# The value projection of a gated linear attention layer by seven products: where its steps stand between the q and k items, and when the sums of x are made

## The chip, the cores and the metric

The kernel runs on one core of one Trainium2 chip. The metric is the device time of one execution in microseconds. The kernel before took 1250.46 us (median of 3 runs, 1249.15 to 1251.29). A difference of 0.2%, 2.5 us, is about what a measurement of it can tell from no change.

The core's engines have names in the profile: PE multiplies matrices (PEld is its weight load), DVE works on vectors, ACT evaluates functions and copies, POOL works on vectors too and issues DMAs that can add to what is in memory, SP only issues DMAs. Each engine takes its instructions in the order that the build leaves: that of the program, in which a scheduler moves what is not held in place.

## The reference

Two layers, each a token mixer and a channel mixer (a gated feed-forward block with a short convolution). The change lies in the first mixer, gated linear attention, and in the reading of x ahead of it.

```python
def gla_mixer(x, w_in, w_gk2, b_gk, norm_w, w_out):
    proj = x @ w_in                                  # x: 512 x 1024
    q, k, v, gate, gk_lr = jnp.split(proj, [hk, 2 * hk, 2 * hk + hv, 2 * hk + 2 * hv], axis=-1)
    gk = jax.nn.log_sigmoid((gk_lr @ w_gk2 + b_gk).astype(jnp.float32)) / GLA_NORMALIZER
    ...
    o = rms_norm(gla_chunked(qc, kc, vc, gc), norm_w)
    o = from_head_chunks(o).astype(x.dtype)
    return (o * jax.nn.silu(gate)) @ w_out
```

All of it is float32. q and k have 4 heads of 128 columns each, v and gate 1024 columns, gk_lr 16.

## The kernel before, in words

**Two parts for each number.** A float32 matrix is kept as a high part in a rounded format that PE takes fast and a low part, the rest: xh and xl for x, wh and wl for a weight. A product is three matmuls: wh xh, wh xl and wl xh. To make a weight ready, a DMA brings the raw tile, ACT casts it to wh (L343, L285) and DVE subtracts to get wl (L346, L286). For some items the low part is made another way (L336 to L338): ACT casts wh, ACT writes minus the raw tile, rounded, into wl (L337), and POOL issues a DMA that adds the raw tile to it (L338); the plan says which items, by its argument `bydma`.

**Start.** x comes in four blocks of 128 tokens (tb 0 to 3). PE transposes a block (`tr4`, tile xT), ACT and DVE make xh and xl from it (`x_parts`). Blocks 0 and 1 come first; `second()` is a task that does blocks 2 and 3 while PE is already at work on the first weights. The first four q and k items (i0 to i3) run on the first half of the tokens, then on the second half. The build keeps its own clock, `self.clk`, an estimate; a task says with `yield` how long it sleeps on that clock, so such numbers and the order of the statements fix where a task's instructions come among the others.

**The order of the GLA projection.** After i0 to i3, the string `GLA_ORDER` fixes the order of PE's work: an `i` is an item, an `s` a step of the value projection. The first `i` is the narrow gk_lr item ("lr" below), the others are i4 to i7, each 24 matmuls of 512 columns (tile fm). In the middle of an item or a step the task `prepare(hd)` puts one matmul for the decay of a head (tile z) and after it a chain on ACT and DVE: z, na (exp and ln on ACT), a scan on DVE (bc), differences and exponentials e1, e2, e4, e5 and bc on ACT, and products with q and k on DVE.

**v by seven products.** x and the columns of w_in for v are cut in 2 by 2 blocks. Instead of 8 block products there are 7, with sums of x's blocks on one side and of the weight's blocks on the other. The weight's sums are made by DMAs on POOL that add to a tile in place (L243, tile wq); x's sums are tiles sf and x1. Its 14 steps s0 to s13 are `sums_proj`: s0 to s3 are the first phase, s4 to s7 the second, s8 to s11 the third, the last two the fourth. A step is 12 matmuls of 512 columns. A phase adds into two pairs of PSUM banks, A and B (tile tm). When its last step is done, `onto_v` reads the banks: for v's first parts by ACT (L1170, tile v), for the others by DVE (L1172). The next phase goes on adding in bank A and B, without clearing, so its first matmul in a bank may only come after that read.

**x's sums.** `x_whole` makes xh + xl of blocks 0 and 1 by four additions on POOL (tiles x1), ahead of the transposes of blocks 2 and 3. `x_sums`, called from `x_parts` right after each transpose, forms x1 minus the even chunks of the transpose (sf "3") and minus that minus the odd ones (sf "2") on DVE. `x_split` adds them to the x1 tiles and makes the high and low parts (tiles sh and sl) that the steps read.

**How far ahead weights are made ready** is `self.look`: 3 at the start, set to `LOOKAHEAD` = 2 by `second()` once blocks 2 and 3 are done, and by `gla` after the items. High and low parts have 4 buffers each, raw tiles 3.

The lines that the prediction names: L180 is every matmul, L191 every transpose, L598 a split in high and low part, L650 the additions on POOL, L660 and L661 the sums on DVE, L678 and L683 the additions of `x_split`, L285, L286, L336 to L338, L343 and L346 the weights' parts, L243 the adding DMAs, L313 a load of a raw tile for the products behind v, L1131 the exponential e1, L1170 ACT's reads of the banks. The change shifts line numbers behind x_sums by 4 at most.

Of the kernel before, what the change touches and what calls it, by code (L numbers as in the profile page):

```python
# [13 lines left out]
ALU = mybir.AluOpType  # L14
# [15 lines left out]
GDN_SCALE = 128.0 ** -0.5  # L30
CHUNKS = ((0, 3), (3, 6), (6, 9))
PLAIN = (9, 11)
GLA_ORDER = "iississsisssissssss"
HALF = 2 * P
AHEAD = 3
BYDMA = 1
# [3 lines left out]
LOOKAHEAD = 2  # L40
TAIL = 4
HEADSTART = 4
# [9 lines left out]
def c4(t):  # L52
    return t.rearrange("p (c i) -> p c i", c=4)


def pairs(t):
    return t.rearrange("p (c i) -> p c i", c=2)


def blk(i, n=P):  # L60
    return slice(i * n, i * n + n)


class Trunk:
# [565 lines left out]
    def x_parts(self, tb):  # L630
        for hf in range(2):
            ps = self.psum("xT")
            self.tr4(ps, self.h[tb][hf])
            xs = (slice(None), slice(4 * hf, 4 * hf + 4), blk(tb))
            self.split_out(self.xh[xs], self.xl[xs], c4(ps))
            if tb > 1:
                self.x_sums(ps, tb - 2, hf)
        self.set(("x", tb))

    def x_whole(self):  # L640

        nc = self.nc
        self.x1 = []
        self.sf = [{k: self.slot("sf") for k in "23"} for _ in range(2)]
        for hf in range(2):
            row = []
            for odd in range(2):
                t = self.slot("x1")
                at = slice(None), slice(4 * hf + odd, 4 * hf + 4, 2), slice(0, HALF)
                nc.gpsimd.tensor_add(pairs(t), self.xh[at], self.xl[at])  # L650
                row.append(t)
            self.x1.append(row)

    def x_sums(self, ps, j, hf):

        nc = self.nc
        p3 = c4(ps)
        even, odd = p3[:, 0::2, :], p3[:, 1::2, :]
        at = slice(None), slice(None), blk(j)
        nc.vector.tensor_sub(pairs(self.sf[hf]["3"])[at], pairs(self.x1[hf][0])[at], even)  # L660
        nc.vector.scalar_tensor_tensor(pairs(self.sf[hf]["2"])[at], pairs(self.sf[hf]["3"])[at], -1.0, odd,  # L661
                                       ALU.mult, ALU.subtract)

    def x_split(self):

# [28 lines left out]
    def load_x(self, x):  # L694

        nc = self.nc
        self.h = [[self.slot("h") for _ in range(2)] for _ in range(NTB)]

        def load(eng, tb):
            for hf in range(2):  # L700
                self.tc.keep_in_program_order(eng.dma_start(self.h[tb][hf], x[blk(tb), blk(hf, S)]))

        def constant(n):
            for _ in range(n):
                self.tc.keep_in_program_order(nc.tensor.matmul(ps, self.ident, self.reset, start=True, stop=True))

        load(nc.sync, 0)
        load(nc.scalar, 1)

        _, w, col, _ = self.plan[0]  # L710
        self.raw = self.rp.tile([P, 1024], F32, name=self.uid("raw"), tag="raw")
        for i, eng in enumerate((nc.sync, nc.scalar)):
            self.tc.keep_in_program_order(eng.dma_start(
                self.raw[:, blk(i, S)].rearrange("p (c f) -> p c f", c=NC // 2),
                w[blk(i, S), col:col + P].rearrange("(c p) f -> p c f", p=P)))

        self.tc.keep_in_program_order(nc.scalar.copy(self.warm, self.one))
        ps = self.psum("warm")
        constant(2)
        self.hold = True  # L720
        for tb in range(2):
            self.x_parts(tb)
        constant(2)
        self.tc.keep_in_program_order(nc.sync.dma_start(self.mark[:, 0:1], self.h[0][1][:, 0:1]))
        self.look = 3
        self.prefetch()
        for tb in range(2, NTB):
            load(nc.sync, tb)
        self.hold = False

        def second():
            self.x_whole()
            yield 5.5
            for tb in range(2, NTB):
                self.x_parts(tb)
                yield 1.2
            self.look = LOOKAHEAD
            yield 4.0
            self.h = [[None] * 2 for _ in range(NTB)]
            yield from self.x_split()  # L740

        self.spawn(second(), 0.5)

    def reload(self, x):

# [296 lines left out]
    def gla_plan(self, w_in, w_out):  # L1042
        items = iter([base + hd * P for hd in range(GH) for base in (0, 512)])
        sums = self.sums_plan(w_in, range(0, NC, 2), 1024)
        for k, kind in enumerate("i" * HEADSTART + GLA_ORDER):
            if k == HEADSTART:
                self.plan_rep(w_in, 3072)
            elif kind == "i":
                self.plan_fm(w_in, next(items), k > HEADSTART + 2)
            else:  # L1050
                self.plan.append(next(sums))
        for hf in range(2):
            for cp in range(NC // 2):
                self.plan_tm(w_in, 2 * cp * P, 2, 2048 + hf * S)
        self.plan_out(w_out, 0, NC, TAIL)
# [29 lines left out]
    def gla(self, x, li, g, b):  # L1085
# [92 lines left out]
        def steps():  # L1178
            self.wait("combined")
            yield from self.sums_proj(self.xs, onto_v)  # L1180
            self.xs = None

        self.look = 3
        self.fm_items(items, steps(), GLA_ORDER)
        self.look = LOOKAHEAD
# [565 lines left out]
```

## Time and profile before

| | us |
|---|---|
| median of 3 runs | 1250.46 |
| the profiled execution | 1254.08 |
| its span, first to last instruction | 1252.4 |
| PE busy in the span | 1233.4 |
| DVE busy | 878.3 |
| ACT busy | 641.9 |
| POOL busy | 188.6 |

How to read it: the profile is one execution, 3.6 us longer than the median of the runs, and 1.7 us of it lie outside the span. PE is busy nearly all the time, so what counts are the few places where PE waits, and those where its clock is halved. The view of the waits names, for each engine and line, whom it waited for, the sum in us, how often, and the longest. The windows give the busy time of each engine in a stretch and the granted clock of PE (PEclk, 1.00 is full). The timeline lists instructions in order of time as start, duration, engine, line, operation, tiles, with the idle time before and what ended it in brackets; x2 means that two such instructions follow each other. A duration in the timeline overlaps the next by about 0.1 us on ACT and DVE and 0.16 us on PE, so start to start is what one costs in a row.

### The profile page before, as it was taken

The page shows a single profiled execution, that of the slowest core. Times are in us where ns is not written, and L with a number is a line of the kernel's source. Part 1 is how long each engine was busy: PE and PEld are TensorE (multiplying, and loading weights), DVE is VectorE, ACT ScalarE, POOL GpSimd, SP SyncE. Part 2 cuts the span into 40 slices and gives each one's busy share as a digit, 9 for nine tenths or more (in the row PEclk, how much of TensorE's full clock was granted, in tenths as well). Part 3 has the DMA queues.
Part 4 walks back from the last instruction along what each step waited for, and adds up shares of the span by engine and source line. Part 5 has one row for each costly group of instructions (what it writes and reads, how often), then busy time and mean ns, then how long its engine had stood idle before and what let it go on. Part 6 is the DMA issues. An engine that isn't in the chain of part 4 may idle for free.

```text
span 1252.4 us, 17852 instructions
## 1 busy us (share of the span) xinstructions
PE 1233.4 (98%) x6512; PEld 1041.5 (83%) x6512; DVE 878.3 (70%) x1717; ACT 641.9 (51%) x1205; POOL 188.6 (15%) x264
## 2 busy tenths in 40 slices
PE   8989999999999999999999999999999999999997
PEld 7868888988888888888888889988888888888885
DVE  6667466588667666687698946669588766766677
ACT  3765443654454454555558745543554454453441
POOL 6230000012101101201013330200012201201201
PEclk9989999999999999999999999999999999999999
DMA  8882324069757756742345950333159666766923
GB/s 221 200 171 79 110 71 148 2 156 222 176 136 167 168 137 168 169 125 96 86 141 134 213 124 27 115 105 114 39 129 229 141 158 169 154 148 152 216 85 101
DMA packets 188679, 172.19 MB, mean 137 GB/s; under 512 B 19240, under 2 KB 142954, under 8 KB 188592
## 3 DMA queue, kind: packets, MB, share of 16 engines
q1 hardware_dynamic: 163728, 117.07, 31.2%
q0 software_dynamic: 23904, 53.07, 23.4%
q8 instruction: 51, 0.84, 0.3%
q10 hardware_dynamic: 960, 0.92, 0.2%
q14 instruction: 36, 0.29, 0.1%
HBM read 148.99 MB, written 5.78 MB: 124 GB/s over the span
## 4 chain that ended last, share of the span: by engine, by line
PE 94%; DVE 3%; DMA 1%; ACT 1%; issue 0%; SPq 0%; DVEq 0%; ACTq 0%
PE fm L180 53%; PE tm L180 31%; PE o L180 2%; PE xT L191 1%; PE R L180 1%; PE V L180 1%; PE yT L191 1%; PE pq L180 1%; PE pg L180 1%; PE vn L180 1%; DVE wl L346 1%; DMA raw<-in_ffn_w_in_dram 1%; PE qs L180 0%; PE s L180 0%; PE ks L180 0%
## 5 line engine op out<-in xcount | busy, mean ns | idle before, releaser
L180 PE MATMUL fm<-xh,wh 128*128 128x512 f32 (+1 forms) x1104 | 407.3, 369 | 0.1
L180 PE MATMUL fm<-xl,wh 128*128 128x512 f32 (+1 forms) x1104 | 402.9, 365 | 0.0
L180 PE MATMUL fm<-xh,wl 128*128 128x512 f32 (+1 forms) x1096 | 399.2, 365 | 1.8 <-DVE wl L346 1.8
L180 PEld LDWEIGHTS fm<-xh,wh 128*128 128x128 f32 x1104 | 208.9, 189 | 33.5 <-ACT wh L343 0.3
L180 PEld LDWEIGHTS fm<-xl,wh 128*128 128x128 f32 x1104 | 209.0, 189 | 32.9 <-issue 0.2
L180 PEld LDWEIGHTS fm<-xh,wl 128*128 128x128 f32 x1096 | 207.0, 189 | 34.9 <-DVE wl L346 2.0
L346 DVE TENSOR_TENSOR wl<-raw,wh 128x1024 fp32r<-128x1024 f32 (+1 forms) x115 | 141.8, 1236 | 113.6 <-ACT wh L343 112.6
L343 ACT CAST wh<-raw 128x1024 fp32r<-128x1024 f32 x113 | 118.7, 1051 | 184.6 <-PE fm L180 103.5
L285 ACT CAST wh<-wq 128x512 fp32r<-128x512 f32 x154 | 91.1, 619 | 106.2 <-PE fm L180 38.3
L928 DVE SCALAR_TENSOR_TENSOR conv<-fm,ffn_cw,conv 128x511 f32<-128x511 f32 (+1 forms) x176 | 131.1, 746 | 19.8 <-ACT conv L926 17.8
L286 DVE TENSOR_TENSOR wl<-wq,wh 128x512 fp32r<-128x512 f32 x154 | 103.2, 686 | 53.9 <-ACT wh L285 52.9
L243 POOL DMA_DIRECT2D wq<-in_ffn_w_out_dram x72 | 63.1, 907 | 264.8 <-DVE wl L286 151.9
L338 POOL DMA_DIRECT2D wl<-raw x31 | 27.4, 884 | 400.3 <-ACT wl L337 384.0
L180 PE MATMUL tm<-wh,gh 128*128 128x512 f32 x216 | 84.0, 389 | 0.0
L180 PE MATMUL tm<-wh,gl 128*128 128x512 f32 x216 | 84.0, 389 | 0.0
L180 PE MATMUL tm<-wl,gh 128*128 128x512 f32 x216 | 84.0, 389 | 0.0
L526 DVE TENSOR_TENSOR h<-h,tm 128x512 f32<-128x512 f32 x68 | 44.9, 681 | 35.4 <-PE tm L180 35.4
L180 PE MATMUL tm<-wh,xh 128*128 128x512 f32 x152 | 63.4, 418 | 0.0
L926 ACT ACTIVATE conv<-fm,ffn_cw 128x512 f32<-128x512 f32 x88 | 59.9, 683 | 1.3 <-PE fm L180 1.3
L180 PE MATMUL tm<-wh,xl 128*128 128x512 f32 x152 | 59.8, 394 | 0.0
L180 PE MATMUL tm<-wl,xh 128*128 128x512 f32 x152 | 59.7, 393 | 0.0
L1312 DVE SCALAR_TENSOR_TENSOR conv<-fm,gdn_cw,conv 128x511 f32<-128x511 f32 (+2 forms) x72 | 53.4, 745 | 7.3 <-ACT conv L1310 6.5
(325 smaller groups left out, 1964.8 us busy)
## 6 DMA issues: line engine op xcount, KB each, us to landing
raw<-in_ffn_w_in_dram SPq DMA_DIRECT2D x88, 512.0 KB, 4.9
wq<-in_ffn_w_out_dram SPq DMA_DIRECT2D x72, 256.0 KB, 5.6
wq<-in_ffn_w_out_dram POOLq DMA_DIRECT2D x72, 256.0 KB, 5.1
raw<-in_gdn_w_in_dram SPq DMA_DIRECT2D x32, 512.0 KB, 4.2
wl<-raw POOLq DMA_DIRECT2D x31, 512.0 KB, 4.8
raw<-in_gla_w_in_dram SPq DMA_DIRECT2D x15, 512.0 KB, 4.5
h<-in_ln_b_dram POOLq DMA_DIRECT2D x20, 256.0 KB, 6.8
wq<-in_gla_w_in_dram SPq DMA_DIRECT2D x16, 256.0 KB, 4.8
```

The lines of the kernel that those rows point to most:

```text
L180: t = self.nc.tensor.matmul(out, a, b, start=start, stop=stop, skip_group_check=open_group)
L191: t = self.nc.tensor.transpose(out, a, self.ident[:n, :n])
L243: nc.gpsimd.dma_start(t[i], quad(i, r, col), accum_op=ALU.add)
L285: nc.scalar.copy(wh, t)
L286: nc.vector.tensor_sub(wl, t, wh)
L338: nc.gpsimd.dma_start(wl.bitcast(F32), raw, accum_op=ALU.add)
L343: cast = nc.scalar.copy(wh[:, cols], raw[:, cols])
L346: low = nc.vector.tensor_sub(wl[:, cols], raw[:, cols], wh[:, cols])
L526: nc.vector.tensor_tensor(h, h, ps, op)
L926: nc.scalar.activation(a, ps, AF.Identity, scale=tap(2))
L928: nc.vector.scalar_tensor_tensor(a[:, d:], ps[:, :S - d], tap(2 - d), a[:, d:], ALU.mult, ALU.add)
L1312: self.conv = nc.vector.scalar_tensor_tensor(a[:, d:], ps[:, :S - d], tap(3 - d), a[:, d:], ALU.mult, ALU.add)
```

## The change

It moves four things.

- `GLA_ORDER`: item i6 goes from behind s4 to ahead of it, so that an item stands between the first and the second phase, as i7 stands between the second and the third in both.
- `x_sums` no longer needs x1: it takes xh minus the transpose, plus xl (three instructions in place of two), and runs after both transposes; `x_whole` comes after it. So the four additions on POOL go behind the transposes of blocks 2 and 3.
- `second()` no longer sets the look-ahead to 2, so it stays 3 until the items are done. The task starts at 6.0 in place of 0.5 on the build's clock.
- No item of the GLA layer has its low part made by DMA any more: i5, i6 and i7 get theirs by DVE, as i0 to i4.

```diff
-GLA_ORDER = "iississsisssissssss"
+GLA_ORDER = "iissississssissssss"
...
             if tb > 1:
-                self.x_sums(ps, tb - 2, hf)
+                self.xt.append((ps, tb - 2, hf))
...
     def x_whole(self):
...
         self.x1 = []
-        self.sf = [{k: self.slot("sf") for k in "23"} for _ in range(2)]
...
-    def x_sums(self, ps, j, hf):
+    def x_sums(self):
...
-        nc.vector.tensor_sub(pairs(self.sf[hf]["3"])[at], pairs(self.x1[hf][0])[at], even)
-        nc.vector.scalar_tensor_tensor(pairs(self.sf[hf]["2"])[at], pairs(self.sf[hf]["3"])[at], -1.0, odd,
-                                       ALU.mult, ALU.subtract)
+        self.sf = [{k: self.slot("sf") for k in "23"} for _ in range(2)]
+        for ps, j, hf in self.xt:
+            p3 = c4(ps)
+            at = slice(None), slice(None), blk(j)
+            s2, s3 = (pairs(self.sf[hf][k])[at] for k in "23")
+            xh, xl = (x[:, 4 * hf:4 * hf + 4:2, blk(j)] for x in (self.xh, self.xl))
+            nc.vector.tensor_sub(s3, xh, p3[:, 0::2, :])
+            nc.vector.tensor_add(s3, s3, xl)
+            nc.vector.scalar_tensor_tensor(s2, s3, -1.0, p3[:, 1::2, :], ALU.mult, ALU.subtract)
...
         def second():
-            self.x_whole()
-            yield 5.5
+            self.xt = []
             for tb in range(2, NTB):
                 self.x_parts(tb)
                 yield 1.2
-            self.look = LOOKAHEAD
-            yield 4.0
+            self.x_sums()
+            self.xt = None
+            yield 1.5
+            self.x_whole()
+            yield 5.0
             self.h = [[None] * 2 for _ in range(NTB)]
             yield from self.x_split()
 
-        self.spawn(second(), 0.5)
+        self.spawn(second(), 6.0)
...
             elif kind == "i":
-                self.plan_fm(w_in, next(items), k > HEADSTART + 2)
+                self.plan_fm(w_in, next(items))
```

The order in which the instructions stand moves on every engine, from the first transposes to the end of the GLA layer; from the first feed-forward block on it is the same as before.

On PE, at the end of s3 (tiles tm_110 and tm_111 are bank A, tm_115 and tm_116 bank B, fm_152 is item i6), before:

```order
L180 MATMUL tm_116_622<-wl_124_663,sh_83_485 128x512
L180 MATMUL tm_116_622<-wh_123_662,sl_84_486 128x512
L180 MATMUL tm_110_605<-wh_128_703,sh_71_404 128x512
L180 MATMUL tm_110_605<-wl_129_704,sh_71_404 128x512
L180 MATMUL tm_110_605<-wh_128_703,sl_72_405 128x512
L180 MATMUL tm_111_606<-wh_128_703,sh_71_404 128x512
```

And now (tm_118 and tm_119 are bank A, tm_121 is of bank B, z_153 is the decay of head 2):

```order
L180 MATMUL tm_121_643<-wl_124_657,sh_93_536 128x512
L180 MATMUL tm_121_643<-wh_123_656,sl_94_537 128x512
L180 MATMUL fm_152_796<-xh_58,wh_127_680 128x512
L180 MATMUL fm_152_796<-xl_59,wh_127_680 128x512
L180 MATMUL fm_152_796<-xh_58,wl_128_681 128x512
...
L180 MATMUL z_153_825<-lr_39_185,gk2_27_169 128x512
L180 MATMUL tm_118_634<-wh_135_723,sh_77_445 128x512
```

Before, the first matmul of s4 follows at once on the last of s3 and writes the bank that `onto_v` has to read; now the 24 matmuls of i6 and the one of z stand between them.

On ACT, around its reads of the banks after the first phase (v_140 to v_143; wh_144 is s5's weight, wh_150 s6's; e1_139 to bc_137 belong to the decay of head 1), before:

```order
L285 CAST wh_144_767<-wq_122_659 128x512
L1118 ACTIVATE na_132_718<-na_132_718 128x512
L1119 ACTIVATE na_132_718<-na_132_718,one_2_85 128x512
L285 CAST wh_150_800<-wq_87_507 128x512
L285 CAST wh_150_800<-wq_127_700 128x512
L1131 ACTIVATE e1_139_750<-e2_138_748 128x512
L1170 ACTIVATE v_140_753<-tm_110_605 128x512
L1132 ACTIVATE e2_138_748<-e2_138_748 128x512
L1170 ACTIVATE v_141_755<-tm_111_606 128x512
```

And now (wh_140 is s5's weight, wh_150 s6's):

```order
L285 CAST wh_140_749<-wq_122_653 128x512
L285 CAST wh_150_790<-wq_62_335 128x512
L1135 ACTIVATE e1_139_740<-e2_138_738 128x512
L285 CAST wh_150_790<-wq_125_675 128x512
L1136 ACTIVATE e2_138_738<-e2_138_738 128x512
L1140 ACTIVATE e4_142_761<-e4_142_761 128x512
L1146 ACTIVATE e5_143_764<-e5_143_764 128x512
L1147 ACTIVATE bc_137_736<-bc_137_736 128x512
L1174 ACTIVATE v_145_773<-tm_118_634 128x512
L1174 ACTIVATE v_146_775<-tm_119_635 128x512
```

The reads stand behind the exponentials of head 1 in both, in the new order behind all five.

On POOL, from the mask on (x1 tiles are the additions of `x_whole`, gk the weight of the decay, rows its bias, wq the weights of v), before:

```order
L1083 CAST gla_mask_31_176<-maskf_30_172 128x512
L650 TENSOR_TENSOR x1_49_207<-xh_58,xl_59 128x512
L650 TENSOR_TENSOR x1_50_209<-xh_58,xl_59 128x512
L650 TENSOR_TENSOR x1_51_211<-xh_58,xl_59 128x512
L650 TENSOR_TENSOR x1_52_213<-xh_58,xl_59 128x512
L1065 COPY mark_3_86<-h_12_104 128x1
L1067 DMA gk_59_311<-in_gla_w_gk2_dram 16x512 x6
L620 DMA rows_60_319<-in_gla_b_gk_dram 4x128
L243 DMA wq_62_329<-in_gla_w_in_dram 128x512
```

And now:

```order
L1087 CAST gla_mask_31_176<-maskf_30_172 128x512
L1069 COPY mark_3_86<-h_12_104 128x1
L1071 DMA gk_51_285<-in_gla_w_gk2_dram 16x512 x6
L620 DMA rows_52_293<-in_gla_b_gk_dram 4x128
L243 DMA wq_58_325<-in_gla_w_in_dram 128x512
L649 TENSOR_TENSOR x1_64_351<-xh_58,xl_59 128x512
L649 TENSOR_TENSOR x1_65_353<-xh_58,xl_59 128x512
L243 DMA wq_60_330<-in_gla_w_in_dram 128x512
L649 TENSOR_TENSOR x1_66_355<-xh_58,xl_59 128x512
L649 TENSOR_TENSOR x1_67_357<-xh_58,xl_59 128x512
```

The four additions have gone behind the first adding DMA of v's weights, and a second such DMA stands between them.

More of the change, by code (lines that the diff above doesn't have):

```diff
@@ L652, in x_whole @@
             self.x1.append(row)
-    def x_sums(self, ps, j, hf):
+    def x_sums(self):
         nc = self.nc
[L657 to L660, printed above, removed]
-        nc.vector.scalar_tensor_tensor(pairs(self.sf[hf]["2"])[at], pairs(self.sf[hf]["3"])[at], -1.0, odd,
-                                       ALU.mult, ALU.subtract)
+        self.sf = [{k: self.slot("sf") for k in "23"} for _ in range(2)]
[7 more added lines that the diff above has]
+            nc.vector.scalar_tensor_tensor(s2, s3, -1.0, p3[:, 1::2, :], ALU.mult, ALU.subtract)
     def x_split(self):
```

## Prediction

> **What bounds the kernel now.** First the page: the span and the busy times.
>
> ```profile
> span 1252.4 us, 17852 instructions
> PE 1233.4 (98%) x6512; PEld 1041.5 (83%) x6512; DVE 878.3 (70%) x1717; ACT 641.9 (51%) x1205; POOL 188.6 (15%) x264
> ```
>
> PE is busy for all but 19 us. The change neither adds nor takes a matmul, so it can gain only where PE waits or its clock is halved, and lose only by new waits. So I read next the waits of PE, all that there are.
>
> ```profile
> PE tm L180 <- ACT v L1170: 4.2, 1, 4.2
> PE warm L705 <- POOL reset L93: 2.0, 1, 2.0
> PE fm L180 <- DVE wl L346: 1.8, 1, 1.8
> PE xT L191 <- DVE ln_mv L779: 1.3, 1, 1.3
> PE tm L180 <- DVE gl L598: 0.4, 1, 0.4
> ```
>
> The first and third lie in the part that the change reorders. The windows, cut where the granted clock changes, show what follows each (start:end, length, then busy us of PE, PEld, DVE, ACT, POOL, then PEclk, DMA share, GB/s).
>
> ```profile
> 12.47:15.88 3.41, 1.62 (x14) 1.43 (x13) 3.41 (x2) 1.04 (x1) 3.41 (x3) 1.00 1.09 348
> 15.88:19.30 3.42, 3.42 (x19) 3.42 (x18) 1.63 (x2) 1.05 (x1) 3.42 (x3) 0.50 0.70 144
> 63.67:67.08 3.41, 0.50 (x3) 0.08 (x1) 3.02 (x4) 1.39 (x3) 1.41 (x3) 1.00 1.08 198
> 67.08:70.49 3.41, 2.12 (x5) 1.74 (x6) 3.00 (x7) 3.29 (x7) 1.49 (x2) 0.50 1.08 195
> 70.49:73.91 3.42, 3.42 (x9) 2.65 (x9) 2.54 (x7) 1.50 (x4) 0.00 (x0) 0.50 1.04 214
> 882.80:886.20 3.40, 2.08 (x12) 1.59 (x12) 2.82 (x12) 1.56 (x3) 0.00 (x0) 1.00 0.34 103
> 886.20:889.60 3.40, 3.40 (x23) 2.97 (x22) 2.40 (x5) 3.40 (x11) 0.00 (x0) 1.00 0.00 0
> ```
>
> After the stretch with 1.62 us of PE work comes half clock for 3.42 us; after that with 0.50 us two such stretches. The 1.3 us wait at 883 left 2.08 us of work in its stretch, and the clock stayed. So each of the two waits costs itself and a slow stretch.
>
> **The change part by part: i6 between s3 and s4.** The timeline of PE at the long wait, and one row of the chain of waits with s0 and s1 for the price of a matmul:
>
> ```profile
> 47.59 5.44 PE tm L180 x24
> 63.78 0.39 PE L180 MATMUL tm<-wh,sl 128*128 128x512 f32 x1
> 68.37 0.80 PE L180 MATMUL tm<-wh,sh 128*128 128x512 f32 x1 [4.20 <-ACT v L1170]
> 73.66 0.52 PE L180 MATMUL fm<-xh,wh 128*128 128x512 f32 x1
> ```
>
> A matmul costs 5.44/24 = 0.227 us from start to start. The next one was due at 64.01 and came at 68.37: 4.36 us. The 12 from there to 73.66 took 5.29 us where 12 x 0.227 = 2.72 are due: 2.6 us more by the half clock. What held it is on ACT:
>
> ```profile
> 64.21 1.14 ACT L285 CAST wh<-wq 128x512 fp32r<-128x512 f32 x2 [0.28 <-PE tm L180]
> 67.20 0.63 ACT L1131 ACTIVATE e<-e 128x512 f32<-128x512 f32 x1 [1.85 <-DVE e L1128]
> 67.73 0.58 ACT L1170 ACTIVATE v<-tm 128x512 f32<-128x512 f32 x1
> 68.21 0.62 ACT L1132 ACTIVATE e<-e 128x512 f32<-128x512 f32 x1
> 68.73 1.56 ACT L1170 ACTIVATE v<-tm 128x512 f32<-128x512 f32 x3
> ```
>
> The reads of the banks stand behind an exponential of head 1, which waits for its chain on DVE. In the new order PE has 24 matmuls of i6 and one z to do meanwhile, 25 x 0.227 = 5.7 us. Let T be the end of s3. ACT then has, one behind the other, a cast that waits for T, e1, a cast, e2, e4, e5 and bc, and then the reads. They follow each other at 68.73 - 68.21 = 0.52 us, so the first read ends at T + 8 x 0.52 = T + 4.2, needed at T + 5.7: 1.5 us to spare. It is less if e1 again waits for DVE. There e1 needs the low part of i6 (now on DVE), na, z, a scan, four low parts of 512 columns and a difference. By these rows,
>
> ```profile
> 33.13 1.23 DVE L346 TENSOR_TENSOR wl<-raw,wh 128x1024 fp32r<-128x1024 f32 x1 [1.16 <-ACT wh L343]
> 51.41 1.22 DVE L1123 TENSOR_TENSOR_SCAN bc<-reset,z 128x512 f32<-128x512 f32 x1
> 55.61 0.69 DVE L1147 TENSOR_TENSOR e<-e,qk 128x512 f32<-128x512 f32 x1
> 56.21 0.68 DVE L1148 TENSOR_TENSOR e<-e,qk 128x512 f32<-128x512 f32 x1
> ```
>
> that is 1.15 + 1.14 + 7 x 0.60 = 6.5 us (0.60 from 55.61 to 56.21, the long ones less 0.08 of overlap). Head 1's z now comes at the end of i5, some 7 us ahead of T, not within s2; following the rows from there, e1 begins about T + 1.2 in place of T + 0.5, and 0.8 us are left. So the wait goes, 4.36 + 2.6 = 7.0 us, with 0 to 0.8 us of a new one at that place. What is next late there would be the second read, 0.5 us behind the first and wanted 0.7 us after it, so none.
>
> **The additions leave DVE alone at the start.** The other wait is for DVE's low part of i1. The chain, DVE's and POOL's timelines, and the durations of the additions (min, median, max in ns):
>
> ```profile
> 12.15 2.27 DVE wl L346
> 12.15 4.48 DVE L346 TENSOR_TENSOR wl<-raw,wh 128x1024 fp32r<-128x1024 f32 x2 [1.59 <-ACT wh L343]
> 12.05 6.95 POOL L650 TENSOR_TENSOR x<-xh,xl 128x512 f32<-128x512 f32 x4
> L650 POOL TENSOR_TENSOR x<-xh,xl x4: 1266/1767/2260, 12.1 to 17.7; 128x512 f32<-128x512 f32 x4
> ```
>
> The low part that took 1.23 us at 33.13 with POOL idle takes 2.27 beside the additions, and it is on the path. Now POOL waits there for x's last block, so the low part takes 1.23: the wait shrinks by 1.04 us to 0.8. The stretch 12.47 to 15.88 then holds 1.62 + 1.04 = 2.66 us of PE work, more than the 2.08 that kept its clock at 883, so the half clock of 15.88 to 19.30 goes as well: 3.42/2 = 1.7 us. Together 2.7 us, after which PE is earlier by that much.
>
> The Trainium skill, "TensorE: Matmul & The Clock Gate", section "What's actually happening", says that the clock drops after at least one idle window of about 3.4 us. The row of 12.47 has 1.62 us of work and was still followed by half clock, so the measurement decides here; the rule is a rival below.
>
> **x's sums and the tight place behind them.** The additions now follow POOL's first adding DMA. One row of the chain of waits, and rows of the timelines and groups:
>
> ```profile
> 45.97 0.23 PE z L180
> 26.57 0.91 POOL L243 DMA_DIRECT2D wq<-in_gla_w_in_dram x1 [2.86 <-DMA wq<-in_gla_w_in_dram]
> 18.41 1.67 DVE L346 TENSOR_TENSOR wl<-raw,wh 128x1024 fp32r<-128x1024 f32 x1 [1.79 <-ACT wh L343]
> 28.81 0.87 POOL L243 DMA_DIRECT2D wq<-in_gla_w_in_dram x1 [1.33 <-DMA wq<-in_gla_w_in_dram]
> L660 DVE TENSOR_TENSOR sf<-x,xT 128x256 f32<-128x256 f32 x4 | 1.7, 414 | 0.0
> ```
>
> From 26.57 less 0.4 (its load is issued behind the low part of 18.41, which took 1.67 us beside an addition and now takes 1.23), two DMAs of 0.9 and four additions of 1.27 to 1.77 end at 33.1 to 35.1. DVE's own additions in x_split wait for them, and behind those stand the low part of i4, eleven rows of 512 columns and a small copy, the last of them gk_lr's correction, which z of head 0 needs: 0.6 + 1.15 + 11 x 0.6 + 0.1 = 8.5, so 41.6 to 43.6. PE, 2.7 us earlier, wants it at 45.97 - 2.7 = 43.3. So 1.7 us to spare up to 0.3 us of wait. The extra instruction per block of x_sums, 4 x 0.33 us (0.41 less overlap), lies ahead of that in DVE's wait for POOL and costs nothing unless the additions come early.
>
> **Low parts by DVE, weights three ahead.** Removed: three ACT passes of 1 us and three adding DMAs. Added: three low parts of 1.15 us on DVE.
>
> ```profile
> 59.71 1.06 ACT L337 ACTIVATE wl<-raw 128x1024 fp32r<-128x1024 f32 x1
> SPq L313 <- DMA wl<-raw: 45.2, 3, 17.5
> ```
>
> SP's queue waited 45 us for those DMAs, with v's loads behind it, but PE never waited for a load there, so that gain is nothing. The 3.5 us on DVE for i6 and i5 are in the two places above; that for i7 has eight steps' cover. A third weight ahead puts s6's cast ahead of the reads, which is counted. From s8 on nearly everything stands as before and only comes earlier; of PE's five waits none lies in the rest of this layer, so nothing. For all new waits I take 0.3 us of 0 to 1.1.
>
> **The sum.** Against the profiled execution: 4.36 + 2.6 + 1.04 + 1.7 - 0.3 = 9.4 us off 1254.08, 1244.7. The median of the runs is 3.6 us lower. The halved stretches are whole lengths of 3.42 us whose grid falls differently against the waits in each execution, so that the 1.8 us wait need not lie in one of them; of the clock's 4.3 us I take 3.1 for the median: 4.36 + 1.04 + 3.1 - 0.3 = 8.2, so 1250.46 - 8.2 = 1242.3. A measurement of this kernel can tell about 0.2%, 2.5 us, from no change.
>
> **The rivals.**
>
> The wait stays at s4. Now five exponentials and more casts stand ahead of all four reads, and 0.8 us of spare is worked out through some 20 rows. Half of it left, 2.2 us with its slow stretch: only 2.1 (start, with two thirds of its clock) + 2.2 = 4.3 off, 1246.2. All of it: 2.1 off, 1248.4, no change that can be told. For: it was ACT's order that made it. Against: i6 gives 5.7 us.
>
> The slow stretch at 15.88 has another cause than the wait and stays. Then 1.1 of the 8.2 is missing (two thirds of 1.7): 1243.4. For: PE had still worked 1.62 us of that stretch. Against: it begins just behind that wait, and the clock is full elsewhere but behind the long one. By the Trainium skill's rule above, 1.8 us would be too short to halve the clock, which makes this case.
>
> Slower: POOL's additions come late. POOL's adding DMAs wait for a landing before they are issued, and the x1 additions now stand behind two. The longest such wait:
>
> ```profile
> POOL wq L243 <- DMA wq<-in_gla_w_in_dram: 11.1, 3, 6.9
> ```
>
> With 6.9 us at each in place of 2.9 and 1.3, and 2.26 us for each addition beside DVE's in place of 1.5, the last one ends 4.0 + 5.6 + 3.0 = 12.6 later than the middle of my range, z of head 0 waits 12.6 less the 0.7 to spare there, 11.9 us, with a slow stretch of 2.6 after it: 14.5 - 8.2 = 6.3 slower, 1256.8. It decides against the change from 5.6 us of wait at z, where 5.6 + 2.6 is the 8.2 gained. Against: both loads are issued from 20 us on and had landed by 28.8.
>
> **How the numbers follow.** Forecast 0.72, the slow stretch that stays 0.10, half the wait at s4 0.06, all of it 0.07, slower 0.05. Faster by over 0.2% (under 1248.0): 0.72 + 0.10 + 0.06 = 0.88; within 0.07; slower 0.05. The range: below, the full clock terms and no new wait, 1250.46 - 9.7 = 1240.8, less the 1.1 us by which the runs scatter, 1239.7; above, the half wait, 1246.2, and 0.8 of scatter, 1247.0.
>
> **What would show it.** Right: no wait of PE for v at L1174, i6 between s3 and s4; DVE's low part at 12.15 near 1.23 us and PE's wait there near 0.8; the clock at 1.00 from 15 to 75 us; PE's waits for z or wl under 1 us together. Wrong: a PE wait for ACT's v or for DVE's lr over 1.5 us with half clock behind it, POOL's last addition ending beyond 36 us, or slow stretches without a wait.

## The result: about 5 us faster, 3 us less than forecast

The changed kernel takes 1245.72 us, the median of 7 runs (1244.55 to 1249.33), beside 1250.47 us for the kernel before (7 runs, 1249.15 to 1251.29): a ratio of 0.9968 with a 95% interval of 0.9956 to 0.998. The profiled execution takes 1248.02 us against 1254.08. So it is faster, by 4.75 us at the median and 6.1 between the two profiled executions, where 8.2 and 9.4 were forecast.

First the page of the changed kernel: its span, and busy time of each engine.

```profile
span 1246.0 us, 17856 instructions
PE 1229.9 (99%) x6512; PEld 1037.7 (83%) x6512; DVE 884.5 (71%) x1724; ACT 638.2 (51%) x1202; POOL 182.6 (15%) x261
```

PE is idle for 16 us in place of 19, and busy for 3.5 us less: the same matmuls at a fuller clock. Next the windows of the changed kernel at the times of the stretches that the prediction showed of before (columns as there: busy us of PE, PEld, DVE, ACT, POOL, then clock, DMA share, GB/s).

```profile
12.47:15.88 3.41, 2.65 (x23) 2.65 (x23) 1.93 (x2) 1.05 (x1) 0.52 (x2) 1.00 1.10 355
15.88:19.30 3.42, 3.42 (x32) 3.42 (x32) 0.88 (x1) 1.96 (x4) 3.20 (x7) 1.00 1.21 251
63.67:67.08 3.41, 3.41 (x17) 2.82 (x16) 3.41 (x8) 2.64 (x6) 0.85 (x1) 1.00 1.03 238
67.08:70.49 3.41, 2.91 (x13) 2.08 (x12) 3.29 (x8) 3.41 (x8) 1.72 (x2) 1.00 1.13 204
70.49:73.91 3.42, 3.42 (x17) 2.84 (x16) 2.41 (x5) 3.39 (x6) 2.16 (x4) 1.00 1.10 172
```

None of these is at half clock any more, and the 2.65 us of PE work in the first is the 2.66 of the prediction. Now PE's waits.

```profile
PE xT L191 <- DVE ln_mv L783: 1.2, 1, 1.2
PE tm L180 <- ACT gh L598: 0.8, 1, 0.8
PE fm L180 <- DVE wl L346: 0.8, 1, 0.8
PE tm L180 <- ACT v L1174: 0.5, 1, 0.5
PE vT L191 <- ACT conv L1318: 0.5, 1, 0.5
...
PE z L180 <- DVE lr L1101: 0.3, 1, 0.3
PE tm L180 <- DVE wl L346: 0.2, 1, 0.2
```

The 4.2 us for v are down to 0.5, and the start's 1.8 to 0.8, as forecast. New are the waits for lr (z of head 0), for wl (the first gate weight), and two far behind the change, for gh at 553 us and conv at 673 us. What they cost was read by taking each PE instruction's start in the changed kernel less that of the same instruction before. That difference is -2.7 us after the start, falls by 0.58 to -2.1 at z of head 0, reaches -9.2 where the wait at s4 was, and gives back 0.82 at s4's new wait, 0.51 at the gate weight, 0.23 at 125 us, and 1.45 at 553 and 673 us; it is -6.3 at the end. In two more profiles of the changed kernel (below) z moved PE by 1.0 and 1.1 us and s4 by as much as here. A wait costs more than its row says: 0.3 at z moved PE by 0.58, 0.5 at s4 by 0.82, because the row counts from the modelled end of the matmul before, which lasts 0.39 us while the next could start 0.23 us after it.

The two late waits are not in every execution of the change: in those two more profiles neither shows. One for gh (0.2 to 0.8) is in five of the ten profiles here that have the new sums and in none of the six with the old, so that a link with the sums is not excluded. The wait for ln_mv, also in code that nothing touched, was 1.3 and 0.9 in two profiles of before and 1.2, 0.7 and 0.7 in three of after. Such waits scatter by execution.

### The profile page after: what moved, and what is told of

The parts are those of the page before. It is cut to its first block, busy times and chain, and to the rows that moved or that the text cites. A ratio compares the mean times of both kernels' runs of the same rounds, so it can differ in the third digit from the quotient of the medians.

```text
span 1246.0 us, 17856 instructions
## 1 busy us (share of the span) xinstructions
PE 1229.9 (99%) x6512; PEld 1037.7 (83%) x6512; DVE 884.5 (71%) x1724; ACT 638.2 (51%) x1202; POOL 182.6 (15%) x261
## 4 chain that ended last, share of the span: by engine, by line
PE 88%; DVE 6%; DMA 2%; ACT 2%; issue 1%; POOL 0%; SPq 0%; DVEq 0%; ACTq 0%
PE fm L180 48%; PE tm L180 30%; PE o L180 2%; PE xT L191 1%; DVE wl L346 1%; PE R L180 1%; PE V L180 1%; DVE conv L1316 1%; PE yT L191 1%; PE pq L180 1%; PE vn L180 1%; DMA raw<-in_ffn_w_in_dram 1%; DVE dt L1375 0%; DVE wl L286 0%; PE qs L180 0%
## 5 line engine op out<-in xcount | busy, mean ns | idle before, releaser
L343 ACT CAST wh<-raw 128x1024 fp32r<-128x1024 f32 x116 | 121.7, 1050 | 188.2 <-PE fm L180 106.4
L338 POOL DMA_DIRECT2D wl<-raw x28 | 24.1, 860 | 396.2 <-ACT wl L337 364.9
```

Of the source, the lines that this page charges most:

```text
L338: nc.gpsimd.dma_start(wl.bitcast(F32), raw, accum_op=ALU.add)
L343: cast = nc.scalar.copy(wh[:, cols], raw[:, cols])
```

## The experiments

Theory: moving i6 makes the gain, its wait and its half clock; what is missing went into new waits, made by GpSimd's additions standing beside VectorE. Rivals: the new sums or the low parts carry part of the gain; or the start term was never worth what the profile showed.

**The noise first.** Kernel before again, unchanged.

> The kernel before, unchanged, for a second profile and the granted clock of each timed run. Theory A (the clock's terms were taken too large for the median): in the timed runs less than the 10.2 us of half clock of the first profile ahead of the last stage falls on PE's work, so runs differ in granted clock and the quick ones, near 1249, show 0.996 or more; a second profile has the two waits of 1.8 and 4.2 us again but one of the slow stretches shorter or missing. Theory B (the first profile is typical): every run has 0.994 and the second profile both slow stretches in full.

1250.66 us (12 runs), ratio 0.9994 (0.998 to 1.0008), span 1250.0. Of its waits and of its timeline:

```profile
PE tm L180 <- ACT v L1170: 4.2, 1, 4.2
...
PE fm L180 <- DVE wl L346: 1.4, 1, 1.4
```

```profile
12.20 4.37 DVE L346 TENSOR_TENSOR wl<-raw,wh 128x1024 fp32r<-128x1024 f32 x2 [0.68 <-ACT wh L343]
```

The wait at s4 is the same and is again followed by two half-clock stretches; the start's is 1.4, with full clock behind it. So the half clock at the start is not in every execution.

> The changed kernel, unchanged, for a second profile. Theory A (the waits at 553 us, 0.8, and at 673 us, 0.5, come from transfers that land at other times in each execution): they are of another size or missing, by 0.5 us or more in sum, while z of head 0, s4 and the first gate weight wait again 0.2 to 0.6 each. Theory B (they come from the change, by another phase of the transfers): all five are there again within 0.2 us. Median 1245.7 in both.

1246.41 us (6 runs), ratio 0.9949 (0.9934 to 0.9964), span 1244.4; a third time, beside the experiments further down:

> The changed kernel once more, beside the three others on this chip: 1246.2 (1245.7 and 1246.4 so far), waits for lr 0.3 to 0.7, for v at s4 0.5, and one VectorE addition at x_sums of 3 to 7 us beside GpSimd's additions.

1246.54 us (6 runs), ratio 0.9968 (0.9957 to 0.998), with 0.9 us of wait for lr and 0.5 for v. At the medians the gain is 4 to 5 us in each of the three.

**i6 alone.** The kernel before with only the order changed:

```
-GLA_ORDER = "iississsisssissssss"
+GLA_ORDER = "iissississssissssss"
```

> The kernel before with the new GLA_ORDER alone. Theory A (the 4.4 us wait was one of order, and goes with i6 between): wait for v at most 0.5, no slow stretch behind it, 4.4 + 1 to 2.6 us off, about 1244.5 to 1246. Theory B (the order alone only moves the wait, and the weights three ahead or the low parts are what clears it): 2 us or more of wait for v or for a weight stay at s4, 1248 or more.

1245.8 us (6 runs), ratio 0.9947 (0.9931 to 0.9963): all of the gain. Its timeline at s4, and a window:

```profile
64.41 0.63 ACT L1131 ACTIVATE e<-e 128x512 f32<-128x512 f32 x1 [1.70 <-DVE e L1128]
64.94 0.58 ACT L1170 ACTIVATE v<-tm 128x512 f32<-128x512 f32 x1
65.42 0.62 ACT L1132 ACTIVATE e<-e 128x512 f32<-128x512 f32 x1
65.94 1.56 ACT L1170 ACTIVATE v<-tm 128x512 f32<-128x512 f32 x3
```

```profile
60.00:74.00 14.00, 14.00 (x63) 11.52 (x62) 11.15 (x20) 11.87 (x22) 5.74 (x8) 1.00 1.06 216
```

ACT still stands at an exponential for VectorE (1.70 us) with the reads of v behind it, as before; PE has i6 to do meanwhile and is busy for all of the 14 us. Against before_again, PE's starts move by -6.84 us here: the 4.36 + 2.6 = 7.0 of the prediction.

**The sums alone,** in the old order and with two weights ahead:

```
-                self.x_sums(ps, tb - 2, hf)
+                self.xt.append((ps, tb - 2, hf))
...
-        self.spawn(second(), 0.5)
+        self.spawn(second(), 6.0)
```

> The kernel before with the new x_sums, x_whole and second() alone (order, look-ahead of 2 behind the transposes and low parts by DMA as before). Theory A: DVE's low part of i1 takes 1.23 in place of 2.27, 1.0 us off, and the slow stretch of 15.9 to 19.3 goes where it falls, so 0.5 to 1.7 more: 1248 to 1249.4; the wait for v at s4 stays at 4 us. Theory B (the late additions take it back): a wait of 1 us or more for z of head 0 or the first step, 1250.5 or more.

1251.41 us (12 runs), ratio 0.9999 (0.9986 to 1.0012): nothing. Of its waits:

```profile
PE tm L180 <- ACT v L1175: 4.7, 2, 3.6
...
PE fm L180 <- DVE wl L346: 0.8, 1, 0.8
```

PE is 0.95 us earlier after the start than in before_again, and s4 takes that back, where PE now waits twice, 4.7 us in all.

**Where the new waits come from.** Three versions of the changed kernel and one between the two kernels. In adds_mid GpSimd's additions come ahead of its first adding DMA:

```
                 yield 1.2
+                if tb == 3:
+                    self.x_whole()
...
-            yield 1.5
-            self.x_whole()
-            yield 5.0
+            yield 6.5
```

> The changed kernel with x_whole called behind the second of the six x_parts: POOL's four x1 additions stand ahead of its first adding DMA, behind the gk copies; the look-ahead of three and VectorE's low parts stay. Theory A (POOL's additions behind the adding DMA, and VectorE's addition of xh, xl beside them, are what made z of head 0 late): no addition at x_sums over 1.5 us (7.0 us in after_again), POOL's last addition ends before 27 us, PE's wait for lr 0 in place of 0.3 to 0.7, PE about 0.9 us earlier from there on; the waits for v at s4 (0.5) and for the first gate weight's low part (0.2) stay. Time 1245.4, that is 1.0 under the changed kernel. Rival (z is late because of VectorE's extra instructions and low parts): the wait for lr stays at 0.3 to 0.7 and the time at 1246.4.

1249.56 us (12 runs, 1244.11 to 1251.66), ratio 0.998 (0.9966 to 0.9993): 3 us the wrong way. The wait for lr is gone, as expected, and a new one is there:

```profile
PE fm L180 <- DVE wl L346: 3.0, 1, 3.0
```

```profile
18.48 5.51 DVE L346 TENSOR_TENSOR wl<-raw,wh 128x1024 fp32r<-128x1024 f32 x1 [3.54 <-ACT wh L343]
...
18.62 0.52 POOL L620 DMA_DIRECT2D rows<-in_gla_b_gk_dram  x1
19.15 5.98 POOL L649 TENSOR_TENSOR x<-xh,xl 128x512 f32<-128x512 f32 x4
```

VectorE's low part of i3, 1.23 us of work, lasts 5.51. GpSimd's first three additions run undisturbed beside it (1.31, 1.28 and 1.26 us one by one) and the fourth, 2.28, ends 1.1 after it. They take turns, and VectorE's came after three of GpSimd's. PE worked for 0.60 us in the stretch from 21.23, and half clock followed it. So my place for the additions was worse than the change's, though three of the 12 runs took 1244.1 to 1245.3 us, as the best versions do, so the stall is probably not in every execution.

The second takes the look-ahead back to two behind the transposes (`self.look = LOOKAHEAD` ahead of `self.x_sums()`), the third brings the adding DMAs back (`k > HEADSTART + 2` as third argument of plan_fm), the fourth does both: it is the new order with the new sums.

> The changed kernel with the look-ahead set back to two behind the transposes; by its code three of POOL's four additions again come ahead of the adding DMA. Theory A: the wait for lr is 0 and the long addition at x_sums under 2.3 us. If the third weight ahead makes the wait for v at s4, that is gone too (1245.0); if the low parts on VectorE or the exponentials ahead of the reads make it, 0.5 us stays (1245.5). The wait for the first gate weight's low part stays at 0.2, since it hangs on VectorE. Rival (look-ahead costs nothing, VectorE's low parts do): all waits stay, 1246.4.

> The changed kernel with the low parts of the last three q and k weights again by ACT and an adding DMA, the look-ahead of three kept. Theory A: the additions still stand behind the adding DMA, so the wait for lr stays at 0.3 to 0.7 us and the long addition at x_sums at 3 to 7 us; the wait for the first gate weight's low part goes, some 0.3 to 0.5 us. Time 1246.0. Rival (VectorE's low parts make z and s4 late): both waits go and the time is 1245.2.

> The kernel before with the new order and the new sums, without the look-ahead of three and with the low parts by adding DMA: the changed kernel less its last two parts. Theory A: start as in the changed kernel (low part at 12.1 us taking 1.23 us, PE's wait 0.8), no wait for lr, none for the gate weight; at s4 0 to 0.5 us. Time 1245.0, 0.8 under the new order alone (1245.8) and 1.4 under the changed kernel. Rival (what the sums give at the start they take back at z in any case): 1245.8 to 1246.4.

Measured: 1246.42 us (5 runs), ratio 0.9965 (0.9952 to 0.9977); 1249.43 (11 runs), 0.9979 (0.9968 to 0.999); 1249.23 (12 runs), 0.999 (0.998 to 1.0). Of the waits expected, a_look2 has none for lr and none for ACT's v (0.3 for VectorE's), a_bydma 0.4 for lr and none for the gate weight. a_look2 is 0.9 to 1.4 us above what was expected, and the last two are 3.4 and 4.2 us above, for a reason that no theory had. The waits of order_sums, and GpSimd's timeline there (its profiled execution, 1252.61 us, is the longest of its 12):

```profile
PE fm L180 <- DVE wl L346: 2.6, 2, 1.8
PE fm L180 <- DMA wl<-raw: 2.3, 1, 2.3
```

```profile
77.33 0.85 POOL L338 DMA_DIRECT2D wl<-raw  x1 [1.65 <-ACT wl L337]
```

The 1.8 us are for i3's low part, held by GpSimd's additions as in adds_mid (4.24 us), again with half clock behind. Then PE waits until 84.63 us for the low part of i7, 7.3 us after GpSimd issued its adding DMA, and another stretch of half clock begins at 84.74; a_bydma has 2.1 us of this wait (issued at 75.99, PE goes on at 82.45), order_only 0.2 (73.35 to 78.79). With the old sums the adding DMA was just in time, with the new ones it is late. So VectorE's low parts, for which I counted no gain, are what the sums need: a_look2 and order_sums differ in them alone, and a_look2 is 2.8 us below. Whether the look-ahead is two or three makes no difference to the time (1246.42 to 1246.54); two moves three additions ahead of the adding DMA, beside i3's low part (4.28 us, wait of 1.7), three moves them behind it, beside a later instruction.

**The additions off GpSimd.** One word in the changed kernel:

```
-                nc.gpsimd.tensor_add(pairs(t), self.xh[at], self.xl[at])
+                nc.vector.tensor_add(pairs(t), self.xh[at], self.xl[at])
```

> The changed kernel with the four x1 additions on VectorE in place of GpSimd, at the same place of the program. Theory B (a VectorE instruction with two operands in SBUF stands still while GpSimd adds: 5.5 and 4.3 us in place of 1.24 for i3's low part in adds_mid and a_look2, 7.0 in place of 0.41 in after_again): no VectorE addition in 17 to 35 us above 1.3 us (128x512 ones 0.7), so four additions of 0.6 us cost VectorE 2.4 us where the stall cost it 6.6; it comes to the correction of lr some 4 us earlier, PE's wait for lr is 0, PE's wait at 21 us is 0. Time 0.6 to 0.9 us under the changed kernel in this call (about 1245.5 beside 1246.2). Rival (the stalls are VectorE's own instructions being slow after a DMA or a PSUM read, whatever GpSimd does): the long instruction stays and the wait for lr at 0.3 to 0.7.

1244.74 us (5 runs, 1244.03 to 1247.57), ratio 0.9956 (0.9943 to 0.9968), 1.8 below the changed kernel measured beside it; four of its five runs lie under all six of the changed kernel's. The timeline of the changed kernel there (after_third), then that of adds_dve:

```profile
26.93 2.86 POOL L649 TENSOR_TENSOR x<-xh,xl 128x512 f32<-128x512 f32 x2
29.43 1.21 POOL L243 DMA_DIRECT2D wq<-in_gla_w_in_dram  x1
30.05 3.15 POOL L649 TENSOR_TENSOR x<-xh,xl 128x512 f32<-128x512 f32 x2
...
27.13 6.50 DVE L363 TENSOR_TENSOR wh<-raw,wh 128x384 fp32r<-128x384 f32 x1 [0.68 <-ACT wh L362]
33.55 0.68 DVE L680 TENSOR_TENSOR x<-sf,x 128x512 f32<-128x512 f32 x1
```

```profile
26.88 0.56 DVE L363 TENSOR_TENSOR wh<-raw,wh 128x384 fp32r<-128x384 f32 x1 [0.65 <-ACT wh L362]
27.36 2.50 DVE L649 TENSOR_TENSOR x<-xh,xl 128x512 f32<-128x512 f32 x4
29.76 0.69 DVE L680 TENSOR_TENSOR x<-sf,x 128x512 f32<-128x512 f32 x1
```

The difference of 128x384 takes 0.56 us alone and 6.50 beside the additions. With them on VectorE it has four more instructions and is 3.8 us further on. Its waits:

```profile
PE fm L180 <- DVE wl L346: 0.8, 1, 0.8
...
PE tm L180 <- DVE wl L346: 0.2, 1, 0.2
```

Neither lr nor v is waited for. PE gains 1.1 us at z and 0.75 at s4. So both waits hang on the additions being GpSimd's, and that is shown. For s4 it is not the only condition: a_look2 and a_bydma keep them on GpSimd and have no wait for ACT's v, but there PE comes to s4 later (68.89 and 68.83 us, beside 67.54 where it was due in the changed kernel). The gate weight's 0.2 stays.

The same with the additions earlier, at `if tb == 2:`, where VectorE stood idle:

> The changed kernel with the four x1 additions on VectorE, called behind the first of the six x_parts, where VectorE stood idle from 15.0 to 18.5 us. Theory B: they take 4 x 0.6 = 2.4 us there, i3's low part keeps 1.24 us and its place near 18.5, the wait for lr is 0 and VectorE runs ahead of PE up to s4. Time 0.8 to 1.2 us under the changed kernel in this call, the best of all (1245.2). Rival (what is gained at lr is lost at s4, where the reads of v stand behind five exponentials): the wait for v at s4 grows from 0.5 to 1.1 to 1.5 us, and the time is that of the changed kernel.

1245.52 us (5 runs, 1245.28 to 1245.94), ratio 0.996 (0.9947 to 0.9974): 1.0 below the changed kernel, not below adds_dve. No wait for lr or v; 0.8 us appears at 88 us, for a copy by VectorE that a transpose needs.

**Low parts and order, without the sums** (order_only, with plan_fm's third argument left out):

> The kernel before with the new order and the low parts of the last three q and k weights on VectorE; the sums and the look-ahead as before. If the waits at s4 (0.5) and for the first gate weight (0.2) come from VectorE's low parts, they are here too, and the time is 1246.3, some 0.5 above the new order alone (1245.8); if they come from the sums being later or from the look-ahead, there is none at s4 (the reads of v stand between the exponentials again), and the time is 1245.8.

1244.26 us (5 runs, 1244.01 to 1244.76), ratio 0.995 (0.9937 to 0.9962). There is no wait for lr or v, and the gate weight's is 0.13: alone, the low parts make none of the two larger waits. All its runs lie under all of the changed kernel's measured beside them (1245.68 to 1247.95), by 2.3 us at the median; the ratio is not distinguishable from that of the order alone.

**The start by itself.** A memset on GpSimd ahead of its additions, in the kernel before and in order_low:

```
+                if not self.x1 and not row:
+                    nc.gpsimd.memset(t, 0.0)
                 nc.gpsimd.tensor_add(pairs(t), self.xh[at], self.xl[at])
```

> The kernel before, with one thing changed: a memset on GpSimd ahead of the four x1 additions, about 0.5 us, so that GpSimd begins them at some 12.6 us and VectorE's low part of i1 (12.15) stands first in every execution. The start term of the prediction alone, in the old order. By the prediction (wait 1.04 and two thirds of the slow stretch's 1.7): 2.1 off, 1248.5. By the theory that the engine that begins first keeps the operands' port and that before's own executions win this race in part of the cases: low part 1.23 to 1.4 us, PE's wait 0 to 0.8, the profile 1.0 earlier at i2, and the median 0.3 to 1.0 off, 1249.6 to 1250.3. If the start is worth nothing: 1250.6. The wait for v at s4 stays at 4.2 with one or two slow stretches after it.

> The kernel before with the new order, the low parts on VectorE, and the same memset ahead of the x1 additions: the best version so far (1244.3) without the race at the start. As order_low already won the race in its profile (low part 11.88, addition 11.99): 1244.0 to 1244.3; if most of its timed executions lost it: 1243.3. The sums, their extra instruction and the look-ahead of three are left out and nothing is lost by it.

start_only: 1250.44 us (11 runs) beside 1251.19, ratio 0.9992 (0.9982 to 1.0001), that is 0.75 us at the median. Its timeline and waits:

```profile
11.88 1.23 DVE L346 TENSOR_TENSOR wl<-raw,wh 128x1024 fp32r<-128x1024 f32 x1 [0.91 <-ACT wh L343]
13.58 2.34 DVE L346 TENSOR_TENSOR wl<-raw,wh 128x1024 fp32r<-128x1024 f32 x1 [0.47 <-ACT wh L343]
...
13.54 6.01 POOL L652 TENSOR_TENSOR x<-xh,xl 128x512 f32<-128x512 f32 x4
```

```profile
PE tm L180 <- ACT v L1172: 4.2, 1, 4.2
...
PE fm L180 <- DVE wl L346: 0.4, 1, 0.4
```

The low part of i1 takes 1.23 us, and PE is 1.24 us earlier behind it than in before_again; at s4 the 4.2 us are all there. order_low_start: 1244.24 us (5 runs), ratio 0.9948 (0.9934 to 0.9961), as order_low without it (1244.26): in that order the start has nothing more to give.

## Why the prediction was right in kind and 3 us too large

**i6 between s3 and s4: right.** It goes by the forecast mechanism, with 6.84 us in the profile for 7.0. What was forecast to stand ahead of the reads stands there in the changed kernel, and the first read misses by little:

```profile
64.44 0.63 ACT L1135 ACTIVATE e<-e 128x512 f32<-128x512 f32 x1 [1.76 <-DVE e L1132]
...
66.54 0.62 ACT L1146 ACTIVATE e<-e 128x512 f32<-128x512 f32 x1
67.06 0.62 ACT L1147 ACTIVATE bc<-bc 128x512 f32<-128x512 f32 x1
67.59 2.03 ACT L1174 ACTIVATE v<-tm 128x512 f32<-128x512 f32 x4
...
67.31 0.40 PE L180 MATMUL z<-lr,gk 96*128 96x512 f32 x1
68.21 0.50 PE L180 MATMUL tm<-wh,sh 128*128 128x512 f32 x1 [0.50 <-ACT v L1174]
```

The 0.8 us to spare were not there. T, the end of s3, is at 61.86, and e1 began at 64.44, 2.6 us behind it where 1.2 was worked out: it waited for VectorE, which came late to head 1's chain and had stood idle for only 1.4 us since 33 us. In adds_dve, where VectorE is ahead, e1 begins 1.8 us behind T (63.02 and 61.22), and PE does not wait.

**New waits, "0.3 us of 0 to 1.1": the step that failed most.** They were 0.58 + 0.82 + 0.51 + 0.23 = 2.1 us in the first profile, beyond the range, and 0.4 to 0.5 more in the other two. At z the chain from GpSimd's last addition to gk_lr's correction was priced at 8.5 us and took 11.0, from 32.5 to 43.5:

```profile
26.95 5.97 DVE L363 TENSOR_TENSOR wh<-raw,wh 128x384 fp32r<-128x384 f32 x1 [0.67 <-ACT wh L362]
29.34 3.15 POOL L649 TENSOR_TENSOR x<-xh,xl 128x512 f32<-128x512 f32 x2
42.82 0.69 DVE L1101 TENSOR_TENSOR lr<-fm,lr 32x512 fp32r<-32x512 f32 x1
```

What I counted as eleven rows behind x_split's first addition are fourteen. The same fourteen stand there in adds_dve, where nothing is held up, so this is a miscount and not work that the stall piled up. The stall itself was priced too low: an addition beside VectorE at up to 2.26 us is the price of one meeting one, and four additions one behind the other held a VectorE instruction for nearly all of them (5.97 us for 0.56). That the extra instruction of x_sums "lies ahead of that in DVE's wait for POOL and costs nothing" held in two of the three profiles; in after_again it is itself what was held, for 7.01 us, and the chain took 11.8. At s4 the wait is that of the late e1 above. For the first gate weight I had taken nothing, because "nearly everything stands as before"; its wait is 0.2 in all three profiles of the changed kernel and 0.13 in order_low, and no kernel with the adding DMAs has it.

**The start, 1.04 us of wait and part of 1.7 us of half clock: probably too large for the median.** The shape was right: low part 1.23, wait 0.8, the clock full. But it rests on which of the two engines begins first. In before VectorE's low part began at 12.15 and GpSimd's addition at 12.05, and VectorE lost 1.04 us; in order_only, with the same start, the low part began at 11.81 and the addition at 12.12, and the addition lost. ACT's cast ahead of it, which waits for the load, began between 10.6 and 11.1 us in the sixteen profiles. In the four with the old start VectorE lost when it began at 11.06 and 11.11 and did not at 10.73 and 10.79. start_only puts the whole term at 0.75 us (-0.1 to 2.3), where 2.1 stood in the forecast; the 2.1 still lies inside that interval. Of the clock's share nothing is seen: the mean granted clock of start_only's runs is 0.9955, as in before's beside them. The half clock at 15.88 was in one of the two profiles where VectorE lost.

**The clock: right at s4.** Of 88 executions of before measured with the experiments, 30 were granted 0.994 or less (median 1253.4 us) and 42 0.996 or more (1250.3); the mean is 0.9953, and 0.9976 in 19 of the changed kernel. The difference is 0.0023 x 1250 = 2.9 us of clock; in the profile 3.4 us of clock (6.83 us at half) cost 2.6 us of time, so 2.9 is worth 2.2. I had taken 3.1 with the start's part in it, 2.0 without.

**The sum with these terms:** 4.36 for the wait at s4 + 2.2 + 0.75 - 2.1 = 5.2 us, where the medians show 4.75, 5.1 and 4.0. The rest, up to 1.2 us, is within the scatter of the runs and is not assigned. Of the 3.0 us between 5.2 and the forecast 8.2, 1.8 are new waits and 1.2 the start with its clock. In the profile, where the start gave its 2.7 us in full, the 3.3 us that are missing of 9.4 are those 1.8 and the 1.45 of the two late waits.

**The rivals.** "The wait stays at s4" is out. "The slow stretch has another cause" was half right: the clock needs more than the wait's length (below). "POOL's additions come late" named the right engine and the wrong price: they were not late (the last ended at 32.5 in the profile, where 33.1 to 35.1 was worked out), but they held up VectorE while they ran.

**The low parts and the third weight ahead: right at nothing for the kernel as it was,** but not in this change: the low parts save the 2.8 us that the sums would cost with the adding DMAs. So of the four parts one makes the gain, two undo each other, and one does nothing that can be measured. What stays open is whether order_low or the order alone is the faster.

## What to carry to other kernels

When two engines get in each other's way, don't price it by one instruction meeting another: count the whole run of instructions that the other engine has queued, and look for what stands on your engine at that time, after the change. A term that depends on which of two events 0.1 us apart comes first is worth only a part of what one profile shows; make a second profile, or take half. And test each part of a change by itself: here one string of the order table, or that with one argument left out, was as fast as or faster than the whole edit.

## What the runs showed of the hardware

**VectorE and GpSimd take turns at two-operand work in SBUF.** Whichever began first mostly kept its time and stretched the other: in order_low VectorE began at 11.88, before GpSimd at 11.99, and took 1.23 us where GpSimd took 2.27; in before it began at 12.15, after GpSimd at 12.05, and took 2.25 where GpSimd took 1.27. But a row of additions kept VectorE out for two to four of them: 4.28, 5.51 and 6.50 us for 1.23, 1.23 and 0.56. The Trainium skill, "SBUF — State Buffer", section "Who interferes with whom", says that a VectorE instruction with two SBUF inputs contends with a GpSimd instruction that reads SBUF, and that the order of issue decides who blocks. These starts agree. Three runs do not: in a_look2, adds_mid and order_sums the low part of i3 began at 18.30, 18.48 and 18.72, 0.6 to 0.7 us ahead of the first addition, and was still held.

**The clock fell when PE had worked for less than about half of one stretch of 3.41 us.** Windows on the stretches of each execution, for a_look2 and for order_sums:

```profile
20.77:24.19 3.42, 1.71 (x15) 1.56 (x14) 3.42 (x5) 0.00 (x0) 2.96 (x2) 1.00 0.08 16
```

```profile
19.88:23.30 3.42, 1.65 (x14) 1.45 (x13) 3.42 (x2) 0.75 (x2) 3.42 (x3) 1.00 0.02 2
23.30:26.71 3.41, 3.41 (x18) 3.41 (x18) 3.41 (x9) 0.00 (x0) 0.80 (x1) 0.50 0.75 228
```

With 1.71 us of work the clock stayed, and in a_bydma with 1.67; with 1.65 it was halved, as in before with 1.62. In the sixteen profiles, cut at each one's own stretches behind the first 6 us, all 24 full-clock stretches with 1.65 us of work or less were followed by half clock, and none with 1.67 or more was. In order_only a wait of 1.8 us at 874 fell across two stretches (2.93 and 2.11 us of work) and cost no clock. So two equal waits differ by where they fall on the grid. At the start, the 1.8 us of before lay in one stretch, while the 1.4 of before_again leave 3.41 - 1.4 = 2.0 us of work wherever they fall, too much for half clock. In sums_only a half-clock stretch with 2.67 us of work was followed by a second one, and in order_sums a full one (3.41) by full clock. By the Trainium skill, "TensorE: Matmul & The Clock Gate", section "What's actually happening", it takes an idle window of about 3.4 us; the rows show that about half of one is enough (1.77 us without work of 3.42 in order_sums), and the measurement decides.
